# A one-core encoder kernel: weights prepared in half pieces behind each softmax, later splits in the first quadrant visits, last squares summed by the tensor engine

## The chip, the cores and the metric

The kernel runs on one core of a Trainium2 chip. The metric is the device time of one execution in microseconds (us); lower is better. A core has five instruction queues that matter here: TensorE (PE, matrix products into PSUM banks of 128x512 floats), VectorE (DVE), ScalarE (ACT), GpSimd (POOL), and SyncE (SP), which in this kernel issues the DMAs. Each queue executes in order: an instruction that waits holds everything behind it on its engine.

## The reference

Two sequences of 512 tokens with 1024 features, each with a memory of 256 rows, go through one layer, and a final norm:

```python
xn = _rmsnorm(x, norm_mix);  mn = _rmsnorm(mem, norm_mem)
u, q, k, v, xq, g = split(xn @ w_in)
y_s5   = state-space branch(u)                       # scan, then gelu and a gated product with w_glu
y_diff = differential attention(rope(q), rope(k), v) # w = softmax(s0) - lam * softmax(s1), 4 heads
y_x    = cross attention(xq, mn @ w_mem_kv)          # 4 heads, 256 memory rows
merged = sum over n of sigmoid(g[n]) * (branch[n] @ w_up[n])
x   = x + merged @ w_out
xn2 = _rmsnorm(x, norm_ffn)
gate, up = split(xn2 @ w_ffn_in)                     # 2 x 2816 columns
x   = x + (silu(gate) * up) @ w_ffn_out
return _rmsnorm(x, norm_final)
```

All of it is in float32.

## The kernel before

**Precision.** A float32 product is made of three products of rounded parts: `split(hi, lo, src)` (lines 123 to 132) writes the rounded part with ScalarE (line 126, or 129 with a scale) and the rest with VectorE (127 or 130). TensorE then adds hi*hi, hi*lo and lo*hi into one PSUM bank (`mm3`, line 145).

**Stages, in order of time.** The state-space branch and its gated product (to about 400 us in the profile), cross attention (to about 523), differential attention with the merge of the branches beside it (to about 880), the output projection and the up-projection (to about 1425), the down-projection in twelve *quadrant visits* (to about 1560), and a remainder of the down-projection with the final norm.

**Cross and differential attention** are written as loops over steps. A step scores 128 queries (`softmax_parts`, line 422: maximum nb, exponentials e by ScalarE at line 431, reciprocal r of their sum at line 435), turns an earlier step's exponentials with TensorE (`ident`), and multiplies with the values. In differential attention two maps are combined: r is scaled (line 759), and VectorE adds the second map into the first (`e`, line 760). Between the parts of a step `fill(n)` takes matrix products off a list `queue` of other work: projections, gates, and, late, the merges (`merge_units`, line 689, whose additions to `mg` POOL makes). From cross attention on TensorE's instructions keep the order in which they are written; for the other engines a scheduler decides it. Rope is `rotated` (lines 661 to 665: VectorE's t from a bank, a shuffle, and two operations on POOL).

**Preparation of the down-projection's weights.** The down-projection uses a seven-product scheme on 2x2 blocks of quadrants, so that it needs three blocks of the weights as they are (A11, A12, A22) and four sums and differences (S1 to S4). The generator `prepare` makes them ahead of time, in 36 pieces: it loads a block of 128x512 (`raw`, two DMAs, lines 500 and 501), POOL makes the four sums (`sums`, lines 505 to 508), each half (three blocks, then four) is split into `hl` (lines 129 and 130) and stored to DRAM (`wD`, line 513). Both halves use one buffer `hl`. The generator is called once for a whole piece, in every second step of cross attention and in every step of differential attention; nothing ties the instructions to a place in their queues, and in the profile they begin at 325 us, before the first softmax, and end at 694.

**Quadrant visits.** `VISITS` lists (output block m, first pair, end pair): visit 0 takes activation pairs 0 and 1, visit 1 pairs 0 to 2, visit 2 pairs 0 to 2, visit 3 pairs 0 to 3. A pair takes 21 matmuls (seven products of three) into seven banks. An activation pair enters with `act_pair` (two loads from DRAM, and the sums `ts`, lines 876 to 879) and `quad_split` (line 886: four splits, of 512, 1024, 1024 and 1024 columns). `quadrants` (line 1008) empties a visit's seven banks: ScalarE copies the first (p, line 1011), VectorE makes seven sums (`summed`, line 1005) and POOL adds the four results to y (line 1103). The two buffers `up` and the two `gf` hold those results. Pair 2 and pair 3 are brought in behind the last sum of the up-projection and of visit 0 (`tc.issue_after(last_sum.ins)`).

**The end.** The last columns are done in three chunks of 512, 256 and 256. For each of eight blocks VectorE adds the product to y (line 1153), ScalarE squares it, POOL (VectorE for the last block) adds the squares into `acc` (line 174). `rstd` sums `acc` over the partitions with matmuls against a column of ones, and the scaled result is stored (line 1131 and 1134).

Of the kernel before, what the change touches and what calls it, by code (L numbers as in the profile page):

```python
# [65 lines left out]
def encoder(ctx: ExitStack, tc: tile.TileContext, a, out):  # L66
# [37 lines left out]
    def aux():  # L104
        return bank("tr")
# [315 lines left out]

    def softmax_parts(pool, col, sc, n, scale, nm, sums=None, bufs=2):


        nb = col.tile([P, 1], F32, tag=nm + "nb", name="nb")
# [5 lines left out]
        S.activation(out=e, in_=sc, func=AF.Exp, bias=nb, scale=scale, accum_out=sm)  # L431
# [63 lines left out]
    def prepare():  # L495
        for m, lo_, hi_ in VISITS:
            for p in range(lo_, hi_):
                raw = pq.tile([P, 4, P], F32, tag="raw", name="raw")
                f = slice(2 * p * P, (2 * p + 2) * P)
                nc.sync.dma_start(raw[:, 1:3], a["w_fo"][m, :, f].rearrange("p (a n) -> p a n", n=P))  # L500
                nc.sync.dma_start(raw[:, 0::3], a["w_fo"][m + 4, :, f].rearrange("p (a n) -> p a n", n=P))
                yield
                a21, a11, a12, a22 = (raw[:, i] for i in range(4))
                s_ = pq.tile([P, 4, P], F32, tag="sums", name="sums")
                PO.tensor_tensor(out=s_[:, 0], in0=a21, in1=a22, op=ALU.add)  # L505
                PO.tensor_tensor(out=s_[:, 1], in0=s_[:, 0], in1=a11, op=ALU.subtract)
# [95 lines left out]
    for i in range(-AHEAD, len(steps) + 1):  # L602
        if i + AHEAD < len(steps):
# [10 lines left out]
            V.tensor_scalar_mul(e, e, r)  # L614
# [24 lines left out]
        if i % 2 == 0:  # L639
            next(prep)  # L640
# [102 lines left out]
    def score(i):  # L743
        h, s, qt = steps[i]
# [15 lines left out]
        V.scalar_tensor_tensor(out=e0, in0=e1, scalar=r1, in1=e0, op0=ALU.mult, op1=ALU.add)  # L760
# [53 lines left out]
    for i in range(-1, n + 3):  # L814
# [193 lines left out]
    def quadrants(ps, p0):  # L1008
# [550 lines left out]
```

## Time and profile before

| | us |
|---|---|
| three runs | 1663.07, 1664.76, 1664.61 |
| their median | 1664.61 |
| the profiled execution | 1669.8 |
| its span, from the first to the last instruction | 1668.0 |
| TensorE busy | 1603.4 |
| VectorE busy | 1151.1 |
| ScalarE busy | 635.5 |
| POOL busy | 532.6 |

Mean granted TensorE clock of the profiled execution: 0.983 of full speed.

How to read the lines of the profile that follow. A line of a timeline gives the start, the duration, the engine, the line of the kernel, the operation with its output and inputs, and in brackets the idle time before it and the instruction that ended it. `x4` stands for four instructions in a row. A line of the waits reads: engine, the operation that waited, the operation that it waited for, then us in total, how many times, and the longest. A line of the windows gives, for a stretch of time, its length, the busy time and instruction count of each engine named in its heading, the granted clock, the share of time in which DMAs ran, and the GB/s moved. A matmul's record is longer than its share of the engine, since matmuls overlap.

### The profile page before, as it was taken

The numbers are of one execution on the slowest core, as the hardware profiler recorded it, in microseconds if no ns is written. First come the engines' busy times: TensorE is split into PE (matmuls) and PEld (weight loads), VectorE is DVE, ScalarE is ACT, GpSimd is POOL, SyncE is SP. The second block draws the span as 40 slices with busy tenths as digits, with TensorE's granted clock in tenths as the row PEclk, the third lists the DMA queues.
The fourth block names the chain that finished last, engine by engine and source line by source line (L and its number), as shares of the span: only waits on it lengthen the run. The fifth ranks groups of instructions, "written<-read, shape, count | busy, mean of one in ns | idle before, by whom it ended". The sixth has DMA issues, their size and how long they took to land.

```text
span 1668.0 us, 21599 instructions
## 1 busy us (share of the span) xinstructions
PE 1603.4 (96%) x7800; PEld 1320.7 (79%) x7800; DVE 1151.1 (69%) x1861; ACT 635.5 (38%) x1130; POOL 532.6 (32%) x446
## 2 busy tenths in 40 slices
PE   7999999899998999999999999999999999899997
PEld 5788788787896778777888877778888888688886
DVE  7957996255665687777455657888777777966445
ACT  6534313246554455656122433223233223221122
POOL 0001100022123444210143344556455553344242
PEclk9999999999998999999999998999999999899998
DMA  9354343869555444334453441222222222787632
GB/s 362 121 165 154 118 138 127 238 214 315 180 185 186 165 158 158 130 127 164 129 181 125 148 125 64 101 101 89 84 81 86 79 88 99 278 289 239 217 117 101
DMA packets 109354, 259.60 MB, mean 156 GB/s; under 512 B 14016, under 2 KB 42432, under 8 KB 109248
## 3 DMA queue, kind: packets, MB, share of 16 engines
q1 hardware_dynamic: 109248, 258.23, 45.8%
q8 instruction: 61, 1.00, 0.3%
q14 instruction: 45, 0.37, 0.1%
HBM read 174.85 MB, written 83.33 MB: 155 GB/s over the span
## 4 chain that ended last, share of the span: by engine, by line
PE 65%; DVE 13%; DMA 10%; issue 4%; ACT 4%; POOL 2%; SPq 1%; DVEq 0%; ACTq 0%; POOLq 0%
PE bkmm L59 56%; DMA wD<-hl 4%; PE bktr L59 3%; DVE wl L127 2%; PE bksc L59 1%; PE bkoo L59 1%; DVE hl L130 1%; PE bktr L62 1%; POOL up L1051 1%; PE bktr L1412 1%; DMA yt<-bD 1%; POOL mg L702 1%; DVE tl L127 1%; ACT hl L129 1%; ACT wh L126 1%
## 5 line engine op out<-in xcount | busy, mean ns | idle before, releaser
L59 PE MATMUL bkmm<-xh,wh 128*128 128x512 f32 x640 | 257.6, 403 | 8.7 <-DVE t L663 6.0
L59 PE MATMUL bkmm<-xh,wl 128*128 128x512 f32 x640 | 252.4, 395 | 2.7 <-DVE wl L127 2.7
L59 PE MATMUL bkmm<-xl,wh 128*128 128x512 f32 x640 | 252.3, 394 | 0.0
L59 PE MATMUL bkmm<-tl,wh 128*128 128x512 f32 (+1 forms) x621 | 243.0, 391 | 3.5 <-DVE tl L127 3.5
L59 PE MATMUL bkmm<-th,wl 128*128 128x512 f32 (+1 forms) x621 | 241.4, 390 | 3.2 <-DVE wl L127 3.2
L59 PE MATMUL bkmm<-th,wh 128*128 128x512 f32 (+1 forms) x621 | 243.1, 392 | 0.0
L126 ACT CAST wh<-wf 128x1024 fp32r<-128x1024 f32 (+1 forms) x133 | 117.6, 884 | 221.8 <-PE bkmm L59 207.8
L127 DVE TENSOR_TENSOR wl<-wf,wh 128x1024 fp32r<-128x1024 f32 (+1 forms) x133 | 143.2, 1076 | 43.9 <-ACT wh L126 39.0
L59 PEld LDWEIGHTS bkmm<-xh,wh 128*128 128x128 f32 x640 | 121.4, 190 | 40.9 <-issue 7.5
L59 PE MATMUL bkmm<-th,w 128*128 128x512 f32 x432 | 142.1, 396 | 6.4 <-DVE up L1005 4.4
L59 PEld LDWEIGHTS bkmm<-xh,wl 128*128 128x128 f32 x640 | 121.2, 189 | 30.9 <-DVE wl L127 4.0
L59 PEld LDWEIGHTS bkmm<-th,wl 128*128 128x128 f32 x621 | 116.8, 188 | 29.6 <-DVE wl L127 5.7
L59 PEld LDWEIGHTS bkmm<-tl,wh 128*128 128x128 f32 x621 | 117.4, 189 | 28.6 <-DVE tl L127 4.7
L59 PEld LDWEIGHTS bkmm<-xl,wh 128*128 128x128 f32 x640 | 121.5, 190 | 22.6 <-issue 0.4
L59 PEld LDWEIGHTS bkmm<-th,wh 128*128 128x128 f32 x621 | 117.4, 189 | 25.0 <-ACT wh L126 1.2
L505 POOL TENSOR_TENSOR sums<-raw 128x128 f32<-128x128 f32 x36 | 20.6, 572 | 358.4 <-DVE zu L395 138.5
L1051 POOL TENSOR_TENSOR up<-up,acc 128x512 f32<-128x512 f32 x44 | 84.6, 1942 | 124.3 <-DVE up L1005 124.3
L59 PEld LDWEIGHTS bkmm<-th,w 128*128 128x128 f32 x432 | 82.5, 191 | 25.5 <-DVE up L1005 5.8
L702 POOL TENSOR_TENSOR mg<-mg,gl 128x1024 f32<-128x1024 f32 x16 | 43.9, 2744 | 139.7 <-DVE gl L698 139.7
L126 ACT CAST wh<-ws 128x1024 fp32r<-128x1024 f32 x44 | 46.1, 1050 | 102.7 <-PE bkmm L59 72.8
L59 PE MATMUL bkmm<-tl,w 128*128 128x512 f32 x216 | 85.2, 395 | 0.0
L431 ACT ACTIVATE e<-bksc,nb 128x512 f32<-128x512 f32 (+1 forms) x96 | 58.6, 613 | 51.3 <-DVE nb L426 34.1
(624 smaller groups left out, 3557.7 us busy)
## 6 DMA issues: line engine op xcount, KB each, us to landing
wf<-in_w_in SPq DMA_DIRECT2D x40, 512.0 KB, 4.1
wD<-hl SPq DMA_DIRECT2D x36, 512.0 KB, 2.6
w<-wD SPq DMA_DIRECT2D x36, 512.0 KB, 4.4
wD<-hl SPq DMA_DIRECT2D x36, 384.0 KB, 2.6
w<-wD SPq DMA_DIRECT2D x36, 384.0 KB, 3.2
gD<-gt SPq DMA_DIRECT2D x24, 512.0 KB, 3.7
gl<-gD SPq DMA_DIRECT2D x24, 512.0 KB, 3.6
wf<-in_w_fg SPq DMA_DIRECT2D x22, 512.0 KB, 3.5
```

What stands on the lines that cost most here:

```text
L59: return self.put(self.eng.matmul(*args, **kw))
L62: return self.put(self.eng.transpose(*args, **kw))
L126: h = S.copy(hi, src)
L127: l_ = V.tensor_tensor(out=lo, in0=src, in1=hi.bitcast(F32), op=ALU.subtract)
L129: h = S.activation(out=hi, in_=src, func=AF.Copy, scale=scale)
L130: l_ = V.scalar_tensor_tensor(out=lo, in0=src, scalar=scale, in1=hi.bitcast(F32), op0=ALU.mult, op1=ALU.subtract)
L431: S.activation(out=e, in_=sc, func=AF.Exp, bias=nb, scale=scale, accum_out=sm)
L505: PO.tensor_tensor(out=s_[:, 0], in0=a21, in1=a22, op=ALU.add)
L702: PO.tensor_tensor(out=mg[m], in0=mg[m], in1=gt, op=ALU.add)
L1051: PO.tensor_tensor(out=up, in0=up, in1=accs[s], op=ALU.mult)
L1412: PE.matmul(ps[:, g * P : (g + 1) * P], w_[:, gg * P : (gg + 1) * P], u_[:, 8 * o + gg, :], start=True, stop=True)
```

## The change

It has three parts.

1. **Preparation.** A piece is made in two calls, one for each half. The raw block is loaded by a DMA that stays behind the last weight load on its queue (`queued()`). The first call splits the three blocks that need no sum, and then POOL computes the four sums over the raw block itself; the second call splits those. The two halves have buffers of their own, `hl3` and `hl4`. A half is called once in a cross-attention step and twice in a differential-attention step, behind the latest exponential (`last_x`) and the latest combined exponentials (`last_e`): its instructions may not be put before these.
2. **Quadrant visits.** `c21` and `c12` of a visit go to the pair of `nsq` buffers, not to `up` and `gf`. Pair 2 is loaded and summed without being tied to a sum; its splits come behind the last sum of visit 0, and pair 3 (sums and splits) behind the last sum of visit 1.
3. **The end.** In the last chunk, the squares of the last three blocks are not added into `acc`: TensorE multiplies `acc` (of the first five blocks) and each of the three squares with the ones, into one bank.

```diff
@@ softmax_parts
-        S.activation(out=e, in_=sc, func=AF.Exp, bias=nb, scale=scale, accum_out=sm)
+        last_x = S.activation(out=e, in_=sc, func=AF.Exp, bias=nb, scale=scale, accum_out=sm)
@@ prepare
-                nc.sync.dma_start(raw[:, 1:3], a["w_fo"][m, :, f].rearrange("p (a n) -> p a n", n=P))
-                nc.sync.dma_start(raw[:, 0::3], a["w_fo"][m + 4, :, f].rearrange("p (a n) -> p a n", n=P))
+                with queued():
+                    nc.sync.dma_start(raw[:, 1:3], a["w_fo"][m, :, f].rearrange("p (a n) -> p a n", n=P))
+                    nc.sync.dma_start(raw[:, 0::3], a["w_fo"][m + 4, :, f].rearrange("p (a n) -> p a n", n=P))
                 yield
-                a21, a11, a12, a22 = (raw[:, i] for i in range(4))
-                s_ = pq.tile([P, 4, P], F32, tag="sums", name="sums")
-                PO.tensor_tensor(out=s_[:, 0], in0=a21, in1=a22, op=ALU.add)
-                PO.tensor_tensor(out=s_[:, 1], in0=s_[:, 0], in1=a11, op=ALU.subtract)
-                PO.tensor_tensor(out=s_[:, 2], in0=a11, in1=a21, op=ALU.subtract)
-                PO.tensor_tensor(out=s_[:, 3], in0=a12, in1=s_[:, 1], op=ALU.subtract)
-                for j, w_ in ((4, raw[:, 1:4]), (0, s_)):
+                for j, w_ in ((4, raw[:, 1:4]), (0, raw)):
                     n = w_.shape[1]
-                    hl = pq.tile([P, 4, 2, P], F32R, tag="hl", name="hl")[:, :n]
+                    hl = pq.tile([P, n, 2, P], F32R, tag=f"hl{n}", name="hl")
                     split(hl[:, :, 0], hl[:, :, 1], w_, scale=0.5)
                     nc.sync.dma_start(wD[m][p][:, j : j + n], hl.bitcast(F32))
+                    if j:
+                        a21, a11, a12, a22 = (raw[:, i] for i in range(4))
+                        PO.tensor_tensor(out=a22, in0=a21, in1=a22, op=ALU.add)
+                        PO.tensor_tensor(out=a21, in0=a11, in1=a21, op=ALU.subtract)
+                        PO.tensor_tensor(out=a11, in0=a22, in1=a11, op=ALU.subtract)
+                        PO.tensor_tensor(out=a12, in0=a12, in1=a11, op=ALU.subtract)
+                        yield
+    def half_piece(behind_):
+        with ExitStack() as es_:
+            for i_ in behind_:
+                es_.enter_context(tc.issue_after(i_.ins))
+            return next(prep, None)
@@ cross attention, each step
-            V.tensor_scalar_mul(e, e, r)
+            last_e = last_x, V.tensor_scalar_mul(e, e, r)
...
-        if i % 2 == 0:
-            next(prep)
+        half_piece(last_e)
@@ differential attention, each step
         fill(10)
+        half_piece(last_e)
...
         fill(10)
+        half_piece(last_e)
...
-        next(prep, None)
@@ quadrant visits
-        t_ = ap2.tile([P, L], F32, tag=tag, name=tag, bufs=bufs)
+        t_ = (rp if tag == "nsq" else ap2).tile([P, L], F32, tag=tag, name=tag, bufs=bufs)
...
-        c21 = summed("up", next(ps), u3, 2)
-        return c11, summed("gf", next(ps), u4, 2), c21, c22
+        c21 = summed(other[0], next(ps), u3, 2)
+        return c11, summed(other[1], next(ps), u4, 2), c21, c22
...
+    nxt = act_pair(2)
+
-    with tc.issue_after(last_sum.ins):
-        pair_in()
...
-        c11, c12, c21, c22 = quadrants(ps, next(ps))
+        c11, c12, c21, c22 = quadrants(ps, next(ps), ("nsq", "nsq"))
...
-        for _ in range({0: 1, 3: 2, 4: 1, 6: 1, 7: 1}.get(v, 0)):
-            if v == 0:
-                with tc.issue_after(last_sum.ins):
-                    pair_in()
-            else:
+        if v == 0:
+            with tc.issue_after(last_sum.ins):
+                pairs.append(quad_split(2, *nxt))
+        elif v == 1:
+            with tc.issue_after(last_sum.ins):
                 pair_in()
+        for _ in range({3: 2, 4: 1, 6: 1, 7: 1}.get(v, 0)):
+            pair_in()
@@ the end
-            sum_sq(acc, y[m][:, c : c + n], m == 0, n, V if m == KD - 1 else PO)
-        final(acc, c, n)
+            if c + n < NT or m < KD - 3:
+                sum_sq(acc, y[m][:, c : c + n], m == 0, n, V if m == KD - 1 else PO)
+                continue
+
+            if m == KD - 3:
+                ss = aux()
+                ones(ss, acc, n, start=True)
+            sq = rp.tile([P, L], F32, tag="nsq", name="nsq", bufs=2)
+            S.square(sq[:, :n], y[m][:, c : c + n])
+            ones(ss, sq, n, stop=(m == KD - 1))
+        final(ss if c + n == NT else column_sums(acc, n), c, n)
```

`ones` makes one matmul of 128x1 for each 128 columns, against the column of ones.

More of the change, by code (lines that the diff above doesn't have):

```diff
@@ L743, in score @@
     def score(i):
+        nonlocal last_e
         h, s, qt = steps[i]
@@ L759, in score @@
         V.scalar_tensor_tensor(out=r1, in0=r1, scalar=nlam, in1=sm0, op0=ALU.mult, op1=ALU.mult)
-        V.scalar_tensor_tensor(out=e0, in0=e1, scalar=r1, in1=e0, op0=ALU.mult, op1=ALU.add)
+        last_e = last_x, V.scalar_tensor_tensor(out=e0, in0=e1, scalar=r1, in1=e0, op0=ALU.mult, op1=ALU.add)
         es[i] = e0
@@ L1003, in summed, with quadrants @@
         nonlocal last_sum
-        t_ = ap2.tile([P, L], F32, tag=tag, name=tag, bufs=bufs)
+        t_ = (rp if tag == "nsq" else ap2).tile([P, L], F32, tag=tag, name=tag, bufs=bufs)
         last_sum = V.tensor_tensor(out=t_, in0=p_, in1=other, op=ALU.add)
         return t_
-    def quadrants(ps, p0):
+    def quadrants(ps, p0, other=("up", "gf")):
         p1 = ap2.tile([P, L], F32, tag="p1", name="p1")
@@ L1074, in prepared @@
         res = {}
-        for j, names in ((4, ("A11", "A12", "A22")), (0, ("S1", "S2", "S3", "S4"))):
+        for j, names in ((4, ("A11", "A12", "A22")), (0, ("S3", "S2", "S4", "S1"))):
             tag = ("wf", "wf", "wh", "wl", "wh", "wl")[n_w % 6]
@@ L1123, in encoder, with ones, column_sums, final @@
     PE.on = False
-    def final(acc, c0, n):
+    def ones(ss, sq, n, start=False, stop=False):
+        for t in range(n // P):
+            PE.matmul(ss[:, t : t + 1], sq[:, t * P : (t + 1) * P], onec[:, 0:1], start=(start and t == 0),
+                      stop=(stop and t == n // P - 1))
+    def column_sums(acc, n):
+        ss = aux()
+        ones(ss, acc, n, True, True)
+        return ss
+    def final(ss, c0, n):
         cs = slice(c0, c0 + n)
-        _, bc = rstd(acc, DM, n // P)
+        _, bc = factor(ss, DM, n // P)
         for m in range(KD):
```

3 lines of the change are left out of this document (added).

## The prediction

> **What bounds the kernel now.** I read the page's busy times first, then windows of TensorE, then the waits and the timelines at the places that the change touches.
>
> ```profile
> span 1668.0 us, 21599 instructions
> PE 1603.4 (96%) x7800; PEld 1320.7 (79%) x7800; DVE 1151.1 (69%) x1861; ACT 635.5 (38%) x1130; POOL 532.6 (32%) x446
> ```
>
> TensorE (PE) is busy 1603.4 of 1668.0 us. So a change can win only where TensorE stands idle, or where its clock falls after such a stand.
>
> ```profile
> core 0: us, PE busy (x), PEclk, DMA share, GB/s
> 1440.00:1460.00 20.00, 15.57 (x53) 0.74 0.67 240
> 1460.00:1480.00 20.00, 20.00 (x90) 1.00 0.77 270
> 1442.10:1452.30 10.20, 7.58 (x17) 0.50 0.50 172
> 527.00:538.00 11.00, 6.20 (x15) 0.53 0.47 175
> 580.00:588.00 8.00, 7.21 (x35) 0.79 0.38 127
> ```
>
> The windows give time, TensorE's busy time and the granted clock. From 1460 on it is full at clock 1.00. Just before, around 1442, 10.2 us ran at 0.50: 7.58 us of busy time that would be about 3.79 us at full clock. The same happens near 527 (the passage from cross attention to differential attention) and, more briefly, near 582.
>
> **The change part by part.** *First quadrant visits.* The stall that the second half of the change touches:
>
> ```profile
> 1437.46 1.22 DVE L127 TENSOR_TENSOR tl<-ts,th 128x1024 fp32r<-128x1024 f32 x1
> 1438.60 0.68 DVE L1005 TENSOR_TENSOR u<-bkmm,u 128x512 f32<-128x512 f32 x1
> 1439.20 0.68 DVE L1005 TENSOR_TENSOR p<-bkmm,u 128x512 f32<-128x512 f32 x1
> 1442.73 0.79 DVE L127 TENSOR_TENSOR tl<-fa,th 128x512 fp32r<-128x512 f32 x1
> 1443.43 2.28 DVE L127 TENSOR_TENSOR tl<-fb,th 128x1024 fp32r<-128x1024 f32 x1
> 1445.64 0.68 DVE L1005 TENSOR_TENSOR up<-bkmm,u 128x512 f32<-128x512 f32 x1
> ...
> 1425.59 0.39 PE L59 MATMUL bkmm<-th,w 128*128 128x512 f32 x1
> 1439.33 0.50 PE L59 MATMUL bkmm<-th,w 128*128 128x512 f32 x1 [2.02 <-DVE u L1005]
> 1442.26 0.80 PE L59 MATMUL bkmm<-th,w 128*128 128x512 f32 x1 [1.97 <-DVE up L1005]
> 1446.37 0.80 PE L59 MATMUL bkmm<-th,w 128*128 128x512 f32 x1 [2.46 <-DVE up L1005]
> ...
> 1434.55 0.68 DVE L1005 TENSOR_TENSOR gf<-bkmm,p 128x512 f32<-128x512 f32 x1
> 1442.92 1.72 POOL L1103 TENSOR_TENSOR y<-y,up 128x512 f32<-128x512 f32 x1
> ```
>
> Each row is start, duration, engine, line, operation; the bracket is the idle time before it and what ended it. The seven sums of visit 0 (L1005) empty the banks that visit 1 wants. VectorE has splits (L127) of later activation pairs in front of and among them, so three times TensorE waits for a sum: 2.02 + 1.97 + 2.46 = 6.45 us. In the changed order the three sums of pair 2 are computed before visit 0, its four splits follow visit 0's last sum, and pair 3 (sums and splits) follows visit 1's last sum. Without a split between them the seven sums run at a pitch of 0.60 us (1438.60 to 1439.20; each is 0.68 long, and they overlap) and as fast as visit 0 closes banks; I put the last at about 1437.5, from the second sum's 1434.55 with five more sums (3.0).
>
> What is late next: pair 2's splits cost 0.69 + 3 x 1.22 = 4.35 us (rows 1442.73 and 1437.46, without the company of POOL), so they end near 1441.9. Visit 0 starts at 1425.59 with 42 matmuls; at the full window's 90 in 20.00 us, about 0.226 each, it ends near 1435.1, and visit 1 wants pair 2 after two pairs of 21 matmuls, 9.5 us later: 1444.6. Slack 2.7 us. Pair 3 is wanted only by visit 3, after two more visits: free. The second pair of result buffers only lets VectorE run ahead of POOL's additions to y (1.72 us each). So 6.45 us of idle goes, and with it the half clock that starts at 1442.1: 7.58 x (1 - 0.50) = 3.79. Taken: -10.2 us, the end that the rows give; the other end is 0, if the order of sums and banks makes a new wait of the same size.
>
> The Trainium skill ("TensorE: Matmul & The Clock Gate", What's actually happening) lets the clock fall only after an idle window of about 3.4 us. No single gap here is that long, and yet the row 1442.10:1452.30 shows 0.50; the measurement decides. By the rule the term would be -6.45 and the total 3.8 us less.
>
> *Preparation of the down-projection weights.* 36 pieces in two halves. Counts and sizes stay, four POOL operations per piece now write over the loaded block, and each half size has its own buffer.
>
> ```profile
> ACT hl L129 <- DMA wD<-hl: 76.2, 41, 5.4
> L130 DVE SCALAR_TENSOR_TENSOR hl<-raw,hl x36: 541/559/1651, 333.1 to 689.4; 128x384 fp32r<-128x384 f32 x36
> L130 DVE SCALAR_TENSOR_TENSOR hl<-sums,hl x36: 679/692/1789, 339.8 to 693.8; 128x512 fp32r<-128x512 f32 x36
> PE bktr L62 <- DVE e L760: 3.3, 2, 2.0
> ```
>
> ScalarE stood 41 times, 76.2 us in all, until a half was stored before it could write the next (columns: us, times, longest). That wait goes. But it is ScalarE's idle time; TensorE's own wait for the combined exponentials (e, L760) is 3.3 us in all. A new wait comes: the block is free only after the second half's split, so the first half of a piece waits for a load; the two raw DMAs sit on SP right behind the store that waits for the same split, so nothing more is held there. In the built order 28 halves stay within the first 18 differential steps, and 14 move from before the first softmax into the last 14 steps (merging). Their price if exposed is 14 x 0.63 us of VectorE (the mean of the medians 0.559 and 0.692) = 8.8 us; VectorE's free time covers them (windows below). The stalls that exist:
>
> ```profile
> 575.61 2.22 POOL L664 TENSOR_TENSOR t<-t,rs 128x512 f32<-128x512 f32 x1 [0.63 <-DVE t L663]
> 576.66 1.58 DVE L130 SCALAR_TENSOR_TENSOR hl<-raw,hl 128x384 fp32r<-128x384 f32 x1
> 579.91 0.74 DVE L760 SCALAR_TENSOR_TENSOR e<-e,r 128x512 f32<-128x512 f32 x1
> 580.79 0.63 PE L62 MATMUL bktr<-ident,e 128*128 128x128 f32 x4 [2.03 <-DVE e L760]
> ...
> 535.00:735.00 200.00, 148.11 (x269) 0.98 0.43 147
> 735.00:880.00 145.00, 85.87 (x139) 1.00 0.49 162
> ```
>
> (The last two are VectorE's windows: 74% busy in the first part of differential attention, 59% in the merging part; +8.8 makes 65%.) A half's split took 1.58 us, not 0.56, beside POOL's rotation, and e came late: 2.03 us idle, then 0.79 clock for 8 us, 1.7 us more: 3.7 us a stall. The changed order still puts a split between the reciprocal and e. I take 0, the value between +3.7 (the two waits for e among 28 halves, carried to 14 more: one more stall) and -7.4 (the two gone), since the order around e is as before and VectorE is less busy where the moved halves go. Where preparation leaves the time before the first softmax, one wait can go:
>
> ```profile
> 385.80 0.50 PE L59 MATMUL bkmm<-zh,wh 128*128 128x512 f32 x1 [1.09 <-ACT wh L126]
> ```
>
> ScalarE's queue was behind there; I take half, -0.5 (0 to -1.1).
>
> *Passage into differential attention.*
>
> ```profile
> 526.46 0.33 SPq L638 DMA_DIRECT2D bD<-xosb  x1
> 529.38 0.52 ACT L129 ACTIVATE hl<-raw 128x384 fp32r<-128x384 f32 x1 [2.95 <-DMA wD<-hl]
> 529.94 0.56 DVE L130 SCALAR_TENSOR_TENSOR hl<-raw,hl 128x384 fp32r<-128x384 f32 x1 [5.01 <-ACT hl L129]
> 530.42 0.68 DVE L661 TENSOR_TENSOR t<-bkmm,rc 128x512 f32<-128x512 f32 x1
> 531.80 0.79 PE L59 MATMUL bkmm<-xh,wh 128*128 128x512 f32 x1 [5.99 <-DVE t L663]
> ...
> DMA to landing us min/median/max: 2.0/2.5/7.7
> ...
> wD<-hl SPq DMA_DIRECT2D x36, 384.0 KB, 2.6
> ```
>
> A half waited 2.95 us for the store, and the rotation behind it held TensorE 5.99 us. In the changed kernel that half stands at the same place and waits for its raw load instead (the last two rows, from issue to landing: 2.5 us in the median for the raw block, 2.6 for a store), and the rotation's buffer still waits for the last cross-attention store, issued at 526.46. Taken: 0, between +1 (the store landed 2.95 us into ScalarE's wait; a load can take up to 7.7, but most take near 2.5) and -8.9 (the stand, and the clock's share 6.20 x 0.47 = 2.9, if neither half nor buffer is late).
>
> *Last squares.*
>
> ```profile
> 1658.43 0.43 DVE L174 TENSOR_TENSOR acc<-acc,nsq 128x256 f32<-128x256 f32 x1 [0.61 <-ACT nsq L173]
> 1658.91 1.01 PE L59 MATMUL bktr<-onec,acc 128*128 128x1 f32 x4 [4.08 <-DVE acc L174]
> ```
>
> VectorE's last addition leaves the chain: 1658.91 - 1658.43, -0.5 us. The six added tiny matmuls but two run earlier, while TensorE is idle.
>
> Sum: -10.2 + 0 - 0.5 + 0 - 0.5 = -11.2 us. The profiled execution took 1669.8 us, so 1658.6; it lies 5.2 above the median of the runs, 1664.6, which gives 1653.4.
>
> **The rivals.** (a) More goes: without the wait for stores the passage or the rotation stalls go too. For it speaks the 76.2 us of ScalarE; against it that the half still stands ahead of the rotation and of e. The passage alone: 1653.4 - 8.9 = 1644.5; with the two stalls at e, 1637.1. (b) Slower: the moved halves sit in front of e in the merging steps, where POOL's additions work beside them. The row at 576.66 shows the mechanism, the 59% speaks against it. Each stall is 3.7 us; it decides from (11.2 + 3.3) / 3.7, four stalls, in 14 halves: 1668.2; six give 1675.6. (c) Pair 2's split is late: beside POOL's y additions the 1024-wide split took 2.28, not 1.22 (row 1443.43). With three such and 0.79, 7.6 us, it ends at 1445.1, 0.5 after it is wanted: 1654 if the clock holds, up to 1658 if it falls again. The Trainium skill ("SBUF — State Buffer", Who interferes with whom) makes a rule of it: a VectorE operation with two SBUF inputs and a GpSimd operation that reads SBUF lock each other out for a whole instruction; the trace's 2.28 beside 1.22 agrees. (d) The stall only moves: visit 1 waits for banks as before, because the sums start late (ScalarE's copy p behind pair 2's copies). Then -1.0: 1663.6, the same.
>
> **How the numbers follow.** The forecast with (c) together 0.50, (a) 0.15, (d) 0.10, (b) 0.25. Predicted 1653.4. The range runs from 1641 (the middle of (a)'s two times) to 1670 ((b) with four stalls and a little). For the forecast alone: 1649 to 1660. A difference under 0.2%, 3.3 us, can't be told from none. Faster 0.65, same 0.10, slower 0.25.
>
> **What would show it.** Right: no TensorE gap over 0.7 us between 1425 and 1460 and the clock at 1.00 there; the stand near 525 to 532 still about 6 us; ones matmuls behind ScalarE's square at the end. Wrong: a wait for hl or e in the merging steps, with the clock below 1; or a visit whose wait is ended by a split of pair 2.

## The result, and the profile after

In 20 runs of each kernel the changed kernel takes 1661.57 us in the median (1660.04 to 1664.72) and the kernel before 1667.32 us (1662.88 to 1671.21). The ratio of the runs is 0.9969, with a 95% interval of 0.996 to 0.9978: faster by some 5.2 us (the medians differ by 5.75), about half of the 11.2 that were forecast. (The three runs that the prediction had of the kernel before gave 1664.61.) The profiled execution has a span of 1662.6 us against 1668.0.

The head of the page of the changed kernel:

```profile
span 1662.6 us, 21641 instructions
PE 1602.0 (96%) x7812; PEld 1319.6 (79%) x7812; DVE 1154.2 (69%) x1860; ACT 636.0 (38%) x1130; POOL 532.2 (32%) x444
```

TensorE in windows of it (length, busy time and instructions, granted clock, DMA share, GB/s):

```profile
520.00:540.00 20.00, 10.27 (x32) 0.66 0.50 171
580.00:600.00 20.00, 20.00 (x108) 1.00 0.38 129
600.00:620.00 20.00, 17.02 (x90) 1.00 0.51 181
740.00:760.00 20.00, 18.13 (x94) 1.00 0.73 248
1440.00:1460.00 20.00, 20.00 (x90) 1.00 1.00 394
```

The window from 1440 is full at clock 1.00 where the kernel before had 15.57 us at 0.74: the quadrant stall is gone, as is the one near 582. But there are gaps between 600 and 800 that were not there, and the passage near 530 is no better than it was. TensorE's waits in the changed kernel (us in total, times, longest), and then what ScalarE waited for ahead of a half:

```profile
PE bktr L62 <- DVE rs L191: 10.2, 5, 3.5
PE bkmm L59 <- DVE t L674: 6.7, 1, 6.7
PE bktr L59 <- ACT nsq L1188: 2.3, 1, 2.3
PE bkoo L59 <- ACT xpTh L126: 2.1, 1, 2.1
PE bktr L62 <- DVE e L772: 1.7, 2, 1.1
PE bksc L59 <- ACT e L434: 1.7, 2, 1.4
...
ACT hl L129 <- DMA raw<-in_w_fo: 52.1, 28, 4.4
ACT hl L129 <- POOL raw L517: 37.3, 26, 3.9
```

The waits for u and up (6.45 us before) have no row any more. The wait of a half for the previous store (76.2 us before) is gone too, but on ScalarE 52.1 + 37.3 = 89.4 us of waits for the raw load and for POOL's sums stand in its place.

Where the time went, stage by stage. Each stage is the distance between the starts of two matmuls that both kernels have (the first score of cross attention, the last product of cross attention, the first and the last score of differential attention, and so on), in the profiled execution:

| stage, us | before | after | difference |
|---|---|---|---|
| from the start to the last part of the state-space branch | 302.24 | 304.22 | +1.98 |
| to its gated product | 76.87 | 76.87 | 0 |
| to the first score of cross attention | 36.38 | 33.11 | -3.27 |
| to its last product | 109.93 | 112.65 | +2.72 |
| the passage, to the next projection's matmul | 6.38 | 7.32 | +0.94 |
| to the first score of differential attention | 25.07 | 24.79 | -0.28 |
| to its last score | 229.56 | 233.78 | +4.22 |
| to visit 0 | 639.16 | 639.07 | -0.09 |
| the quadrant visits | 181.41 | 170.58 | -10.83 |
| the rest, to the last instruction | 60.94 | 60.13 | -0.81 |

The quadrant visits end near 1607 us in the profile before, later than the 1560 given for it above. The first row has nothing to do with the change, whose first instructions on an engine come later: among the later kernels with the old preparation it is 301.3 once and 303.2 once, and with the new one between 299.3 and 304.3. Of the others, the quadrants and the end gave 11.6 us, the time before the first softmax 3.3, and cross attention, the passage and differential attention took 7.9 back. Without the first row the stages sum to -7.4 us; the runs, which count for the total, say -5.2.

### The profile page after: what moved, and what is told of

Its sections match the earlier page's. It is cut to its first block, busy times and chain, and to the rows that moved or that the text cites. A ratio compares the mean times of both kernels' runs of the same rounds, so it can differ in the third digit from the quotient of the medians.

```text
span 1662.6 us, 21641 instructions
## 1 busy us (share of the span) xinstructions
PE 1602.0 (96%) x7812; PEld 1319.6 (79%) x7812; DVE 1154.2 (69%) x1860; ACT 636.0 (38%) x1130; POOL 532.2 (32%) x444
## 4 chain that ended last, share of the span: by engine, by line
PE 66%; DVE 12%; DMA 7%; issue 5%; POOL 4%; ACT 4%; SPq 1%; POOLq 0%; ACTq 0%; DVEq 0%
PE bkmm L59 58%; DMA raw<-in_w_fo 4%; PE bktr L59 3%; DVE wl L127 2%; DVE hl L130 1%; POOL up L1064 1%; ACT hl L129 1%; PE bktr L1447 1%; POOL mg L713 1%; PE bksc L59 1%; DMA yt<-bD 1%; DMA aD<-ac 1%; PE bktr L62 1%; ACT e L434 1%; POOL raw L516 1%
## 5 line engine op out<-in xcount | busy, mean ns | idle before, releaser
L59 PE MATMUL bkmm<-xh,wh 128*128 128x512 f32 x640 | 256.8, 401 | 7.9 <-DVE t L674 6.7
L59 PE MATMUL bkmm<-xh,wl 128*128 128x512 f32 x640 | 251.9, 394 | 2.6 <-DVE wl L127 2.6
L59 PE MATMUL bkmm<-xl,wh 128*128 128x512 f32 x640 | 251.8, 393 | 0.0
L59 PE MATMUL bkmm<-tl,wh 128*128 128x512 f32 (+1 forms) x621 | 242.6, 391 | 3.5 <-DVE tl L127 3.5
L59 PE MATMUL bkmm<-th,wl 128*128 128x512 f32 (+1 forms) x621 | 241.2, 390 | 3.3 <-DVE wl L127 3.3
L59 PE MATMUL bkmm<-th,wh 128*128 128x512 f32 (+1 forms) x621 | 242.9, 391 | 0.0
L126 ACT CAST wh<-wf 128x1024 fp32r<-128x1024 f32 (+1 forms) x133 | 117.7, 885 | 236.7 <-PE bkmm L59 221.8
L59 PEld LDWEIGHTS bkmm<-xh,wh 128*128 128x128 f32 x640 | 121.0, 189 | 39.7 <-issue 7.5
L514 POOL TENSOR_TENSOR raw<-raw 128x128 f32<-128x128 f32 x36 | 17.0, 473 | 408.0 <-DVE hl L130 340.1
L59 PEld LDWEIGHTS bkmm<-xh,wl 128*128 128x128 f32 x640 | 120.9, 189 | 30.8 <-DVE wl L127 3.8
L59 PEld LDWEIGHTS bkmm<-tl,wh 128*128 128x128 f32 x621 | 117.4, 189 | 28.8 <-DVE tl L127 4.7
L59 PEld LDWEIGHTS bkmm<-th,wl 128*128 128x128 f32 x621 | 116.6, 188 | 29.5 <-DVE wl L127 5.8
L59 PE MATMUL bkmm<-th,w 128*128 128x512 f32 x432 | 139.0, 389 | 0.0
L59 PEld LDWEIGHTS bkmm<-xl,wh 128*128 128x128 f32 x640 | 121.1, 189 | 22.4 <-issue 0.4
L59 PEld LDWEIGHTS bkmm<-th,wh 128*128 128x128 f32 x621 | 117.3, 189 | 25.0 <-ACT wh L126 1.2
L59 PEld LDWEIGHTS bkmm<-th,w 128*128 128x128 f32 x432 | 81.1, 188 | 17.1 <-DVE up L1018 0.3
L126 ACT CAST wh<-ws 128x1024 fp32r<-128x1024 f32 x44 | 46.1, 1051 | 102.6 <-PE bkmm L59 72.8
L59 PE MATMUL bkmm<-tl,w 128*128 128x512 f32 x216 | 84.0, 389 | 0.0
L59 PE MATMUL bkmm<-yh,wh 128*128 128x512 f32 x192 | 75.9, 397 | 0.3 <-DVE gl L709 0.3
```

The lines of the kernel that those rows point to most:

```text
L59: return self.put(self.eng.matmul(*args, **kw))
L126: h = S.copy(hi, src)
L514: PO.tensor_tensor(out=a22, in0=a21, in1=a22, op=ALU.add)
```

## The experiments

**Apart: quadrants and end with the old preparation, and the new preparation alone.** In `quad_tail` the loop over the visits (with pair 2's splits behind visit 0's sums) and the end are the changed ones, and `prepare` and its calls are the old ones; in `prep` it is the other way round. Against the kernel before, `quad_tail` has

```diff
-        c11, c12, c21, c22 = quadrants(ps, next(ps))
+        c11, c12, c21, c22 = quadrants(ps, next(ps), ("nsq", "nsq"))
...
+                pairs.append(quad_split(2, *nxt))
...
+            ones(ss, sq, n, stop=(m == KD - 1))
```

and `prep` has

```diff
-                for j, w_ in ((4, raw[:, 1:4]), (0, s_)):
+                for j, w_ in ((4, raw[:, 1:4]), (0, raw)):
...
-        next(prep, None)
+        half_piece(last_e)
```

> The kernel before with the quadrant part and the end part of the change, and the old preparation. Theory 1 (the quadrant part gains what was forecast, and the new preparation gives about half of it back): the three waits of TensorE between 1436 and 1447 and the half clock behind them go, -10.2, and the end -0.5 to -1.5: ratio to before about 0.9933, some 5 us faster than the changed kernel. Theory 2 (the preparation is neutral, and the quadrant part gains only half, since what was waited for there is waited for later): ratio about 0.997, the same as the changed kernel.

> The kernel before with the new preparation alone. Theory 1: slower than before by about 5 us, ratio 1.003, with waits of TensorE for rs, e and the passage that total some 5 us more than before between 500 and 800. Theory 2: the same as before, ratio 1.000.

`quad_tail` took 1656.65 us against 1665.81 of the kernel before beside it, ratio 0.9958 (0.9942 to 0.9974); `prep` 1672.64, ratio 1.0048 (1.0035 to 1.0061); theory 1 had 0.9933 and 1.003. In the stages, the quadrant visits took 170.63 and 181.44 us, the rest 60.13 and 60.66. So theory 2 falls: in the stages the quadrants gain what was forecast, and the new preparation alone makes the kernel slower. In the stages the parts also add up, but in the runs they do not: 0.42% faster and 0.48% slower would together leave the time of the kernel before, and the changed kernel is 0.31% faster than it, more than the intervals allow. No run explains that difference.

**Were the halves moved into the merging steps the cause?** `prep_early` was to make 14 halves before the first softmax in the changed kernel.

```diff
     next(prep)
+    for _ in range(14):
+        next(prep)
```

> The changed kernel, but 14 halves are made before the first softmax, so that the merging steps of differential attention have none, as in the kernel before. Theory 1a (the cost comes from the 14 halves that moved into the merging steps, seen as waits at 708 to 782): 4 to 5 us faster than the changed kernel, ratio to before about 0.994. Theory 1b (the cost comes from the new chain of load, split, POOL, split, wherever it runs): same as the changed kernel, 0.997.

1665.17 us, ratio 0.9993 (0.9983 to 1.0004), slower than the changed kernel. But the edit did not do what it was for: the raw loads were still tied to the last weight load, only 4 halves ran before the first score (14 in the kernel before), and the last one ran at 768 us (789 in the changed kernel, 694 in the kernel before). It tells nothing on the question, and was done again below.

**Does the half ahead of the rotation hold the passage?** `no_pass` leaves out the calls in the last cross-attention steps.

```diff
-        half_piece(last_e)
+        if i < 29:
+            half_piece(last_e)
```

> The changed kernel, but no half is made in the last four cross-attention steps, so that none stands ahead of the rotation at the passage (near 532). If the half is what holds the passage: TensorE's wait of 6.69 us there and the one of 2.14 before it shrink to about 2 together, with the half clock gone, 8 us faster than the changed kernel, ratio 0.992. If the rotation's buffer waits for the last cross-attention store in any case, as the prediction had it: the 6.7 us stay near 5 to 6, and the time is within 2 us of the changed kernel.

1662.56 us, ratio 0.998 (0.997 to 0.9991). VectorE at the passage of this kernel:

```profile
528.00 0.69 DVE L130 SCALAR_TENSOR_TENSOR hl<-raw,hl 128x512 fp32r<-128x512 f32 x1 [1.75 <-ACT hl L129]
532.92 0.56 DVE L130 SCALAR_TENSOR_TENSOR hl<-raw,hl 128x384 fp32r<-128x384 f32 x1 [4.23 <-ACT hl L129]
533.40 0.68 DVE L673 TENSOR_TENSOR t<-bkmm,rc 128x512 f32<-128x512 f32 x1
```

The halves are still there: the preparation runs later than its calls, and halves of earlier calls ran here. So this edit could not answer it either.

**Placement or buffers?** `half_old` has the changed kernel's calls by halves, but the old buffers; `buf_new` the old calls by whole pieces, bound to nothing, but the new buffers. Both have the changed quadrants and end. Against the changed kernel, `half_old` has

```diff
-                for j, w_ in ((4, raw[:, 1:4]), (0, raw)):
+                s_ = pq.tile([P, 4, P], F32, tag="sums", name="sums")
+                for j, w_ in ((4, raw[:, 1:4]), (0, s_)):
...
-                    hl = pq.tile([P, n, 2, P], F32R, tag=f"hl{n}", name="hl")
+                    hl = pq.tile([P, 4, 2, P], F32R, tag="hl", name="hl")[:, :n]
```

and against `quad_tail`, `buf_new` has (with the four sums made over the loaded block, behind the first half)

```diff
-                for j, w_ in ((4, raw[:, 1:4]), (0, s_)):
+                for j, w_ in ((4, raw[:, 1:4]), (0, raw)):
...
-                    hl = pq.tile([P, 4, 2, P], F32R, tag="hl", name="hl")[:, :n]
+                    hl = pq.tile([P, n, 2, P], F32R, tag=f"hl{n}", name="hl")
```

> The changed kernel (quadrants and end as changed), with half pieces placed behind the softmax as changed, but with the old buffers: a tile for the sums, and one buffer for both halves. It splits the preparation's cost into placement and buffers. Theory P (placement: halves that stand behind the softmax and in the merging steps are what costs): about the time of the changed kernel, stage from the first to the last score of differential attention near 233 to 235 us, as with the new preparation. Theory B (buffers: each half waits for a load or for POOL because the block is reused in place): near the kernel with the old preparation, ratio to before 0.995 or less, that stage near 228 us.

> Quadrants and end as changed; old placement (a whole piece at a call, bound to nothing), but the new buffers: sums over the loaded block, a buffer for each half size. Theory P: like the kernel with the old preparation, ratio 0.995 or less, differential stage near 228 us, nothing prepared after 700 us. Theory B: like the changed kernel, 0.997, with waits of ScalarE for loads and for POOL of some 80 us, and that stage near 232 or more.

`half_old` took 1659.73 us, ratio 0.9965 (0.9951 to 0.9979); `buf_new` 1656.37, ratio 0.9945 (0.9925 to 0.9965). The stages that differ, with those of later experiments (all of them with the changed quadrants and end, us):

| kernel | buffers | calls | to the first score | cross | passage | differential | last half at |
|---|---|---|---|---|---|---|---|
| quad_tail | old | whole pieces | 35.64 | 110.11 | 6.31 | 227.84 | 691 |
| buf_new | new | whole pieces | 38.37 | 109.95 | 5.44 | 224.35 | 701 |
| half_old | old | halves | 33.11 | 110.07 | 6.25 | 233.94 | 767 |
| after | new | halves | 33.11 | 112.65 | 7.32 | 233.78 | 789 |
| early_old | old | halves, 14 early | 38.14 | 109.97 | 6.12 | 229.17 | 694 |
| early_new | new | halves, 14 early | 39.60 | 112.33 | 7.56 | 231.64 | 712 |
| free | new | halves, unbound | 33.11 | 113.04 | 7.28 | 233.47 | 764 |

Differential attention goes with how late the preparation ends: 228 and 224 us where its last half runs near 700 in the kernels that call whole pieces, 234 where it runs in the merging steps, whatever the buffers. Cut at the first score of the nineteenth of its 32 steps, it is the last fourteen steps that differ: 95.8 us before, 96.0 in `quad_tail` and 94.6 in `buf_new`, against 101.7 in `half_old` and 102.0 in the changed kernel. The new buffers by themselves cost nothing in the runs (0.9945 against 0.9958), although the time before the first score is 2.7 longer and ScalarE waits for loads and POOL in `buf_new` as in the changed kernel (57.7 and 32.4 us). Cross attention and the passage are, in this table, slower only where new buffers and calls by halves come together, early start or not.

**The 14 halves once more.** In `early_old` and `early_new` the first 14 halves' loads are bound to nothing.

```diff
-                with queued():
+                with (queued() if bound[0] else ExitStack()):
...
+    for _ in range(14):
+        next(prep)
+    bound[0] = True
```

> Quadrants and end as changed, halves behind the softmax as changed, old buffers, but 14 halves are made before the first softmax with their loads bound to nothing, so that fewer or none are left for the merging steps. If the 14 moved halves are what the differential stage pays for: that stage falls from 233.9 us (all halves behind the softmax, old buffers) to 230 or less, the stage before the first softmax grows from 33.1 to 35 or 36, and the total is 1 to 3 us faster than that kernel (1659.7): about 1657.5. If the place of every half behind the combined exponentials is what costs: the stage stays near 234 and the total near 1661.

> The same with the changed buffers (sums over the loaded block, two buffers for halves), that is the changed kernel with 14 halves made before the first softmax. If the moved halves cost: differential stage from 233.8 to 230 or less, total some 2 us faster than the changed kernel (1661.6). If the reuse of the block in place costs by itself behind the softmax, the cross-attention stage stays at 112.6 where the old buffers have 110.1, and the passage's waits of 2.1 and 6.7 stay.

`early_old` took 1656.78 us, ratio 0.9927 (0.9911 to 0.9943); `early_new` 1666.72, ratio 1.0 (0.999 to 1.001). With the old buffers it went as expected: differential attention fell from 233.94 to 229.17, and the time before the first score rose from 33.11 to 38.14. By the stages the two cancel (-4.77 and +5.03); the runs say faster, by 3 us if the medians are compared and by 6 if the ratios to the kernel before are. With the new buffers the differential stage fell by 2.1 only (its last fourteen steps to 99.2, with four halves still in them), and the time before the first score grew by 6.5, so the kernel lost 5 us by the medians (its profiled execution was its fastest run). TensorE and VectorE in the merging steps, `half_old` and then `early_old` (columns: PE, PEld, DVE, ACT, POOL busy):

```profile
735.00:800.00 65.00, 62.02 (x314) 47.46 (x314) 48.51 (x89) 38.08 (x87) 4.59 (x9) 0.97 0.64 213
```

```profile
735.00:800.00 65.00, 63.73 (x339) 49.94 (x338) 47.56 (x88) 37.07 (x84) 0.00 (x0) 1.00 0.48 161
```

VectorE is not full in either (48.5 and 47.6 of 65 us), and yet TensorE has 1.7 us less idle time where no half is left, and its clock is 1.00 in place of 0.97. (The two windows are cut at the same times, some 4 us apart in the work.) The last fourteen steps take 95.7 us in `early_old`, 6.0 less than in `half_old`.

**Is it the binding?** `free` is the changed kernel without it.

```diff
             for i_ in behind_:
-                es_.enter_context(tc.issue_after(i_.ins))
+                pass
```

> The changed kernel with its half calls and its buffers, but the halves are bound to nothing: the line that puts them behind the latest exponential and the latest combined exponentials is taken out. If the binding is what makes the two new costs (late halves in the merging steps, and halves that wait for their load or for POOL in front of the last cross-attention work): stages as with the old placement and the new buffers, cross attention near 110, passage 5.4, differential stage 224 to 228, before the first softmax 36 to 38, total about 1656 to 1658. If the half calls themselves cost: cross attention 112.6 and differential stage near 233, total 1661.

1663.34 us, ratio 0.9986 (0.9971 to 1.0001), and every stage as in the changed kernel (last row of the table). So the binding behind the softmax is not the cause, and the first of the two theories falls. Unbound, the first half still runs only at 388 us and the last at 764: it is the late start, not the place behind an exponential, that leaves halves for the merging steps. How a half slows the end of cross attention and the passage is seen in the traces (below); no run took apart further why only new buffers with calls by halves do it.

**The passage again.** In `nsq` (on `quad_tail`) and `best` (on `buf_new`) the output of cross attention that is stored last goes to one of the two `nsq` buffers, which the rotation's buffers don't share; `early_nsq` is the same on `early_old`.

```diff
-            osb = xa.tile([P, L], F32, tag="osb", name="xosb", bufs=1)
+            osb = rp.tile([P, L], F32, tag="nsq", name="xosb", bufs=2)
```

> Quadrants and end as changed, old preparation, and the cross-attention output that is stored last is put into another buffer (one of the two nsq), whose memory the rotation's buffers don't share. The prediction said that the rotation at the passage waits for that last store as well as for the half ahead of it. If so, the rotation's first product runs before the half, TensorE's wait of about 6 us near 530 falls below 3, and with part of the half clock the time falls by 4 to 9 us against the kernel with quadrants, end and old preparation: ratio to before 0.990 to 0.993. If the half alone holds it, nothing changes: the ratio stays near 0.995.

> Quadrants and end as changed, old placement, new buffers, and the last cross-attention output in a buffer that the rotation doesn't share. If the passage's gain (stage 6.25 to 0.23) adds to that of the buffers (differential stage 224.4): 1656.4 - 5 = about 1651, ratio 0.991. If the rotation's earlier start only moves the stall to the next combined exponentials, as it did with the old buffers (a wait of 3.41 near 592): about 1656, ratio 0.994.

> As the first kernel of this group (14 halves early, the others behind the softmax, old buffers), and the last cross-attention output in the other buffer. A half that is bound behind the combined exponentials can't stand ahead of them, so that the wait near 592 should not come: passage near 0.3, differential stage 230 or less, total about 1651 to 1653. If the passage's gain is given back here too: about 1657.

| kernel | median us | ratio to before | passage | differential |
|---|---|---|---|---|
| nsq | 1656.16 | 0.9943 (0.9923 to 0.9964) | 0.23 | 234.41 |
| early_nsq | 1654.89 | 0.9917 (0.9899 to 0.9935) | 0.24 | 230.59 |
| best | 1649.53 | 0.9901 (0.9886 to 0.9916) | 0.23 | 224.62 |

The passage's wait disappears in all three: with other memory for the stored block the first rotation no longer has to wait for the store, and it also runs far ahead of the half in VectorE's queue. In `nsq` it is at 514, in the kernel before at 530:

```profile
514.36 0.69 DVE L661 TENSOR_TENSOR t<-bkmm,rc 128x512 f32<-128x512 f32 x1
```

In `nsq` the 6.1 us were given back. The timeline of that kernel near 592: TensorE, then VectorE and ScalarE just before:

```profile
592.34 0.87 PE L62 MATMUL bktr<-ident,e 128*128 128x128 f32 x3 [3.41 <-DVE e L760]
...
590.11 1.42 DVE L130 SCALAR_TENSOR_TENSOR hl<-raw,hl 128x384 fp32r<-128x384 f32 x1 [1.46 <-ACT hl L129]
591.45 0.74 DVE L760 SCALAR_TENSOR_TENSOR e<-e,r 128x512 f32<-128x512 f32 x1
...
589.55 0.52 ACT L129 ACTIVATE hl<-raw 128x384 fp32r<-128x384 f32 x1 [2.66 <-issue]
```

and TensorE in the window from 590 (busy, clock):

```profile
590.00:600.00 10.00, 7.66 (x31) 0.66 0.45 162
```

ScalarE stood 2.66 us before a half (the profile gives no instruction that ended it), VectorE's part of that half waited for it, and the combined exponentials e stood behind both; TensorE waited 3.41 us for them, and the clock was 0.66 in that window. In `early_nsq` no such wait came, as expected, but against `early_old` the runs gained 2 us of the passage's 5.9, not 4 or more; the differential stage took 1.4 us of it, and no run shows where the rest went. `best`, with the new buffers, has no such wait, and its runs keep what the passage gave, as expected. (Its cross attention took 111.73 us, 1.8 more than in `buf_new`, with new waits of 0.70 and 0.47 us near 419 and 438; these have not been traced.) Its matmuls at the passage follow one another:

```profile
530.07 0.39 PE L59 MATMUL bkoo<-xpTh,mkvl 128*128 128x512 f32 x1
530.30 0.39 PE L59 MATMUL bkmm<-xh,wh 128*128 128x512 f32 x1
```

It is the fastest kernel of the study, 11 to 12 us below the changed one. Its four runs were 1649.3, 1649.4, 1649.7 and 1653.8.

## Why the prediction was right or wrong

**Right: the first quadrant visits.** Forecast -10.2, measured -10.83 in the changed kernel, and 170.6 to 171.1 us for the stage in every kernel that has the part. The last sum of visit 0 ended 12.2 us after the visit began (forecast 11.9). Rival (d), sums that start late, did not come. Rival (c) came close. Pair 2's splits in the changed kernel:

```profile
1443.28 0.68 DVE L1018 TENSOR_TENSOR nsq<-bktr,p 128x512 f32<-128x512 f32 x1
1443.88 0.86 DVE L127 TENSOR_TENSOR tl<-fa,th 128x512 fp32r<-128x512 f32 x1
1444.67 2.31 DVE L127 TENSOR_TENSOR tl<-fb,th 128x1024 fp32r<-128x1024 f32 x1
1446.90 3.45 DVE L127 TENSOR_TENSOR tl<-ts,th 128x1024 fp32r<-128x1024 f32 x2
...
1444.15 3.98 POOL L1116 TENSOR_TENSOR y<-y,nsq 128x512 f32<-128x512 f32 x2
```

They took 6.5 us, not 4.35, and ended at 1450.35. Visit 0 began at 1431.81, so pair 2 was wanted at 1450.8 by the prediction's own count (9.5 + 9.5 us later): the slack was 0.4 us, not 2.7, and that nothing waited was a near thing. (The prediction's 0.226 us per matmul is the spacing of the rows; the 90 in 20.00 us that it names for it would be 0.222.) The prediction had the better price in its own row, 2.28 beside POOL, and took 1.22 without it. The Trainium skill ("SBUF — State Buffer", Who interferes with whom) states that a VectorE operation with two SBUF inputs and a GpSimd operation that reads SBUF lock each other out. The row 2.31, beside POOL's additions to y from 1444.15 on, agrees with it again.

**Right: that the clock's share goes with the stall.** With the 6.45 us of gaps also the half clock went: 1.00 in the window from 1440, where it was 0.74. By the rule of the Trainium skill ("TensorE: Matmul & The Clock Gate", What's actually happening) that the prediction names, an idle window of about 3.4 us, no half clock would have been there to lose; the measurement decides. But gaps do not always bring it: after the 2.87 us wait near 616 in the changed kernel the clock is 1.00 in the windows 600 to 620 and 620 to 650, while before a 2.03 us wait near 581 cost 1.7 us of clock.

**Right in kind: the end.** Forecast -0.5, measured -0.81: the stage up to the last product with the ones shrank by 0.53 (VectorE's addition), and 0.28 more behind it.

**Too small: the time before the first softmax.** Forecast -0.5, measured -3.27: 33.11 in every kernel with at most four halves left there, against 35.6 to 36.4 with the old preparation. The term took half of one wait of 1.09; the wait of 1.55 for sg near 404 goes too, and the changed kernel has no wait left in that stage (the other 0.6 us are not traced).

**Wrong: the step "I take 0" for the preparation.** It rested on VectorE's free time ("74% busy ... 59% in the merging part; +8.8 makes 65%"). The first failure is the window, 735 to 880. In the kernel before the last score is at 787, and only after it VectorE has so much free time, while in the changed kernel 18 halves (one before) ran between 691 and 789. The last fourteen steps and the stretch behind them before, and the last fourteen steps after (columns as above):

```profile
691.20:787.00 95.80, 93.80 (x500) 72.76 (x500) 71.11 (x132) 56.97 (x131) 12.61 (x8) 1.00 0.41 136
787.00:880.00 93.00, 92.79 (x430) 76.23 (x427) 47.00 (x68) 24.61 (x47) 30.01 (x11) 1.00 0.48 159
```

```profile
691.30:793.30 102.00, 95.10 (x499) 72.63 (x500) 81.45 (x148) 65.54 (x148) 31.25 (x44) 1.00 0.63 215
```

So VectorE was 74% busy where the halves went, 51% behind the last score, and it is 80% busy with them, not 65%. The second failure is the price. Measured: differential attention +4.22, that is -2.0 in the first eighteen steps and +6.2 in the last fourteen; `half_old` against `early_old` shows that 4.77 us of the stage hang on the halves left for the merging steps, though VectorE is full in neither. Busy shares do not price an instruction in an ordered queue: it costs when it stands ahead of something that TensorE needs next. TensorE's waits in the last fourteen steps grew from 2.0 to 6.9 us. One of them, on ScalarE and TensorE of the changed kernel:

```profile
705.20 0.53 ACT L129 ACTIVATE hl<-raw 128x384 fp32r<-128x384 f32 x1
705.63 0.69 ACT L434 ACTIVATE e<-bksc,nb 128x512 f32<-128x512 f32 x1
706.42 1.28 ACT L190 ACT_TABLE_LOAD   x1
...
708.19 0.65 PE L62 MATMUL bktr<-ident,rs 128*128 128x128 f32 x4 [2.23 <-DVE rs L191]
```

The half stands ahead of an exponential and of the square root with its table load, and TensorE waits 2.23 us for the end of that row, where it waited 0.76 before. The half's own 0.5 us is a part of the difference; how the rest and the other waits of these steps divide over the halves is not traced.

The changed buffers have a stall of their own, near 616, in the first eighteen steps. ScalarE, POOL and TensorE of the changed kernel:

```profile
611.15 0.63 ACT L129 ACTIVATE hl<-raw 128x512 fp32r<-128x512 f32 x1 [1.77 <-POOL raw L517]
611.69 0.26 ACT L814 ACTIVATE acc<-bktr 128x128 f32<-128x128 f32 x1
...
613.35 0.71 ACT L434 ACTIVATE e<-bksc,nb 128x512 f32<-128x512 f32 x1
614.64 1.28 ACT L190 ACT_TABLE_LOAD   x1
615.94 0.20 ACT L190 ACTIVATE rs<-ss 128x4 f32<-128x4 f32 x1
...
609.26 1.32 POOL L516 TENSOR_TENSOR raw<-raw 128x128 f32<-128x128 f32 x1
...
616.41 0.65 PE L62 MATMUL bktr<-ident,rs 128*128 128x128 f32 x4 [2.87 <-DVE rs L191]
```

A half waits 1.77 us for POOL's sums. Behind it in ScalarE's queue stand the squares of the norm, two exponentials, and the square root with its table load; TensorE waits 2.87 us for the end of that row. `half_old` has no wait there, and `early_new` has the same one (2.86), so it goes with the buffers and not with the late halves; the first eighteen steps are no longer for it, since the stalls that the prediction did look at went as the other end of its bound had it. The wait of 2.03 for the combined e near 581 is gone, and TensorE's waits for the combined e fell from 3.3 to 1.7 us in all. The waits for rs rose in their place, from 6.0 to 10.2.

**Wrong: that nothing changes in cross attention, and the passage.** Forecast 0, measured +2.72 and +0.94. At the end of cross attention the changed kernel has, on ScalarE and then on TensorE:

```profile
522.49 0.52 ACT L129 ACTIVATE hl<-raw 128x384 fp32r<-128x384 f32 x1 [1.56 <-DMA raw<-in_w_fo]
522.92 1.03 ACT L126 CAST wh<-wf 128x1024 fp32r<-128x1024 f32 x1
523.86 0.37 ACT L126 CAST xpTh<-bktr 128x256 fp32r<-128x256 f32 x1
...
524.27 0.49 PE L59 MATMUL bkoo<-xpTh,mkvh 128*128 128x512 f32 x1 [2.14 <-ACT xpTh L126]
534.17 0.79 PE L59 MATMUL bkmm<-xh,wh 128*128 128x512 f32 x1 [6.69 <-DVE t L674]
```

The half that waits for its load has the last transposed exponentials behind it: 2.14 us where the kernel before had 0.95 (its row of the waits, "PE bkoo L59 <- ACT xpTh L126", was 0.9). Two shorter waits, 0.28 and 0.54 us near 507 and 512, are new too; together this is 2.0 of the 2.72. In `half_old` a half waits 1.38 us for a store at the same place, but earlier: ScalarE then still waits 0.57 us for TensorE before the next transposed exponentials, so that the half holds nothing.

At the passage the step that failed is "nothing more is held there", on SP. ScalarE, SP and VectorE of the changed kernel:

```profile
527.57 0.59 ACT L649 COPY xosb<-bkoo 128x512 f32<-128x512 f32 x1 [0.23 <-PE bkoo L59]
...
528.09 0.33 SPq L511 DMA_DIRECT2D wD<-hl  x1
528.59 0.33 SPq L504 DMA_DIRECT2D raw<-in_w_fo  x1
528.97 0.69 SPq L505 DMA_DIRECT2D raw<-in_w_fo  x1
529.76 0.52 SPq L650 DMA_DIRECT2D bD<-xosb  x1
...
532.31 0.56 DVE L130 SCALAR_TENSOR_TENSOR hl<-raw,hl 128x384 fp32r<-128x384 f32 x1 [4.25 <-ACT hl L129]
532.79 0.68 DVE L672 TENSOR_TENSOR t<-bkmm,rc 128x512 f32<-128x512 f32 x1
```

The last output of cross attention is copied by 528.16, but its store goes out at 529.76, 1.6 us later, behind the store of a half and the two raw loads that follow it. In the kernel before it went out as soon as the copy ended (526.46). From there to the landing it took 2.7 us, 3.5 before, so that some 0.8 us of the +0.94 are this; in `half_old` and `buf_new`, too, the store goes out with the end of the copy. For the stand itself the prediction named two holders, the half and the buffer that waits for the last store, and both are there: the store lands near 532.4, and the rotation starts right behind the half at 532.79. The experiments with the other buffer show that the stand goes when the buffer is changed. Since the rotation then also runs ahead of the half, they do not show what either holder alone would cost.

**The rivals.** What came is the mechanism of (b), late halves in front of what TensorE needs, but smaller than its price: in the last fourteen steps waits of 0.3 to 2.2 us without loss of clock in place of 3.7 each, for rs and ScalarE's exponentials as well as for e. In the stages the quadrants and the end give 11.6, and the rest of the change takes a net 4.2 of it (7.9 less 3.3 and small differences); the runs leave 5.2. What the forecast put at nothing, the preparation's cost in differential attention (+4.2) and in cross attention with the passage (+3.7), halved the gain, and the time before the first softmax, which came out 2.8 better than forecast, hid a part of that.

## What to carry to other kernels

Price a moved instruction by what stands behind it in its queue, a DMA queue included, and by what it must wait for there, not by the engine's busy share; and read a busy share only over the stretch where the instruction will run. A buffer that removes one wait may leave another of the same size (a store before, a load and POOL's sums after); only the waits that reach the bound engine count. Where a stage starts with a long wait, look whose memory its first tile takes over: one output put into another buffer freed 6 us of the passage here, but the runs kept them in full only in `best`; in `nsq` the next stage gave them back at once, with a half ahead of the exponentials that come next.

## What the runs showed of the hardware that was not expected

Work that the change does not touch gave stage lengths that differ between the profiled executions: from the start to the last part of the state-space branch 299.3 to 304.3 us. The runs of the kernel before spread over 1660 to 1672.6 us. So differences of 2 us between single profiles say little outside the stages that agree in every kernel. A gap of TensorE of 2.0 us was followed by a lower granted clock at one place, and a gap of 2.87 us was not at another.
